# A two-layer trunk on one core: the pooling branch in pass 1 of the retention, and the first layer's last norm in the scheduler's order

## The chip, the cores and the metric

The kernel runs on one NeuronCore of a Trainium2 chip. The metric is the time of one execution on the device, in microseconds (us). Its engines are named as the profile names them: PE (TensorE, matrix products), DVE (VectorE), ACT (ScalarE), POOL (GpSimd) and SP (SyncE, which here issues DMAs). Each engine runs its own instructions in a fixed order and waits where a semaphore has not been reached yet.

## The reference

The input is a stream of 1024 tokens and 256 context tokens of width 1024, all in float32. Two layers follow each other; each adds two branches to the stream:

```python
for l in range(DEPTH):
    need_ctx = l < DEPTH - 1
    ax = modulate(rmsnorm(h, norm1_g[l]), mx[0], mx[1])
    ac = modulate(rmsnorm(hc, norm1_g[l]), mc[0], mc[1])
    yx, yc = mixing_layer(ax @ w_in[l], ac @ w_in[l], ...)
    h = h + mx[2] * (yx @ w_out[l])
    h = h + mx[5] * conv_ffn(modulate(rmsnorm(h, norm2_g[l]), mx[3], mx[4]), w_up[l], ..., w_down[l])
    if need_ctx:  # the same for hc, with mc and ac
        ...
return rmsnorm(h, final_g)
```

`mixing_layer` splits the projected columns over three kinds of heads: a pooling mixer (four groups of 64 columns, each with a centred mean over 2, 4, 8 or 16 tokens less the token itself, then a 64x64 product and a scale), a neighbourhood attention of six heads on a grid 64 columns wide, and a retention of six heads that runs over chunks of 128 tokens forwards and backwards. The retention rotates queries and keys by position, normalises each head's result and multiplies it by a silu gate. `conv_ffn` is a gated MLP of 2 x 2816 columns with a depthwise convolution over three tokens.

## The kernel before

Activations lie with their features on the 128 partitions and their tokens along the free axis. Tokens are cut in three parts: 0 and 1 are the two halves of 512 tokens of the stream, 2 is the context of 256. The last layer needs no context after its keys and values.

Products that need full precision are taken from pairs: a value is split in a rounded high part and the remainder (`xh` and `xl`, `wh` and `wl`, `ph` and `pl`), and each product is three matmuls, high by high, high by low, low by high (lines 194 to 196 for `gps`, the projections). A projection of one weight tile and one part of 512 tokens is 24 matmuls.

A layer runs like this: first norm, attention (each head's projections, then its softmax), retention, output projection (`ops`), second norm, then the MLP, whose up and down products are written in an order by hand and whose last two of 22 tiles of columns are done by plain down products (`dps`). The next layer's first norm is computed while these end.

**The retention** (`ret`) takes its six heads in three passes of two. A pass p consists of `keys` (load or project keys and values, rotate, transpose: `vps2`, `kps`; scale by decay: `kd`; the chunk sums: `pk`; the recurrence: `S`), `query` and `gate` (projections `gps` of the pass's columns), and `mix` (`pa`, the chunk's scores, `at`, these times a decay mask, `pf`, the query times the state, `py`, the scores times the values, then a norm per head in `tm` and a transpose `yps`).

**The pooling branch** is two calls of `pool_mean` and `pool_out`, for two groups of columns at a time. `pool_mean` loads a tile `pb` with a margin of zeros, adds shifted copies of it into the two halves `sa` and `sb` of a tile `sab` (line 559), corrects the eight columns at each end (572, 573), and writes mean less value back to `pb` (574). `pool_out` multiplies by the group weights (`pps`, line 582), scales on ACT (583) and stores to DRAM (584, 586). Two buffers are shared. `sab` has the tag of `kd`, with one buffer: it can be written when the last `pk` of the `keys` before it has read `kd`. `pb` has the tag of the raw keys and values `kw` and `vw`, with two buffers. The products `pps` and `py` share one PSUM buffer.

**What sets the order.** Outside the MLP a list scheduler places the instructions on each engine when the program is built, from estimated costs; the order in which the code emits them is a priority, not a rule. Inside `order`, a region in manual schedule that begins at the MLP, each engine keeps the order in which the code emits. The tail of the MLP lies inside it: `head(part, between)` emits the down products of one part, its residual `g` or `hd` (`acc_h`) and its squares, and between them the functions handed over, which compute the next norm of the part before: `st` (sums of squares by a product with ones, `nps`, and the power, `rs`), `sp` (the spread over the partitions, `dg` and `npb`), and `modulate` (`nt`, then `xh` on ACT and `xl` on DVE). The first projections of the next layer are `gps` again, and their first user is the copy `vt` on ACT (line 292), which frees the accumulator.

Of the kernel before, what the change touches and what calls it, by code (L numbers as in the profile page):

```python
# [7 lines left out]
F32 = mybir.dt.float32  # L8
F32R = mybir.dt.float32r
AF = mybir.ActivationFunctionType  # L10
# [9 lines left out]
KT = 8  # L20
# [19 lines left out]
NCH = 5  # L40
# [5 lines left out]
def tile_trunk(ctx, tc, xT, ctxT, cc, ccT, w_mod, w_mod0, colp, w_in, pool_bd, rpbU, lgp, w_out, w_up, w_down, fing,  # L46
# [297 lines left out]
    def mixing(l, X, mp):  # L344
# [186 lines left out]
        def ret():  # L531
# [207 lines left out]
            for p in range(3):  # L739
                if p == 0:  # L740
                    tables()
                kk = keys(p)
                q = query()
                gate(p)
                if p == 0:
                    for i in range(2):
                        pool_out(i, pool_mean(i))
                mix(p, *kk, q)
# [10 lines left out]
    def layer(l, X, hsrc):  # L759
# [24 lines left out]
        def hv(k, part):  # L784
            if part == 2:
                return hc[k]
            o, n = PARTS[part]
            return hs[0][k][:, o:o + n]
# [130 lines left out]
        def spread(part, pool, tag):  # L919
            pbs[part] = sums[part].spread(pool, tag)  # L920
# [350 lines left out]
        for ch in range(NCH):  # L1271
            for half in range(2):
                ps = {}
                tail = half == 1 and ch == NCH - 1
                if tail:
                    xpool[0] = wx
                for q in range(2):
                    ps["a", q] = psf.tile([128, 512], F32, tag="a", name="da")
                    bc = psf.tile([128, 1024], F32, tag="bc", name="dbc")
                    ps["c", q], ps["b", q] = bc[:, L], bc[:, R]  # L1280
                uc = {}
                nxt = ch + 1 < NCH
                for i, name in enumerate(names):
                    ui = UNITS.index(name) if name in PRODS else -1
                    if i == 0:
                        load_group(l, NF + 2 * ch + half + 1)
                    if ch == 0 and half == 0:
                        if name == "A11":
                            fetch(0, "T4")
                            reload((4, 5), 0)  # L1290
                            reload((6, 7), 1)
                        elif name == "A12":
                            reload((4, 5), 1)
                            reload((6, 7), 0)
                            if not last:
                                reload(range(4, 8), 2)
                    elif half == 0 and name == "A11":
                        fetch(ch, ops[6])
                    if half == 0 and not last:
                        j = 4 * ch + 4 + i - 3  # L1300
                        if 0 <= i - 3 < 4 and j < NF:
                            fetch_c(j)
                    if nxt and half == 0 and name == "A22":
                        fetch(ch + 1, ops[0])
                    if nxt and half == 1 and 0 <= ui < 6 and ui != 3:
                        fetch(ch + 1, ops[ui + (ui < 3)])
                    if half == 0 and 0 <= ui < 3:
                        convert(ch, ops[4 + ui])
                    if tail and name == "A11":
                        p = NF // 2 - 1  # L1310
                        raw_g = {(i, part): stage(g_dram[p][:, 2 * i + part]) for part in range(2) for i in range(2)}
                    if tail and ui > 2:
                        i, part = (ui - 3) % 2, (ui - 3) // 2
                        gl_[i, part] = pair(GTAG[("B11", "T1")[part]], raw_g[i, part])
                    wh, wl = [t.rearrange("p (k c) -> p k c", k=2) for t in weights()]
                    tick()
                    pop(1)
                    for q in range(2):
                        w = lambda j: (wh[:, j, 128 * q:128 * q + 128], wl[:, j, 128 * q:128 * q + 128])
                        if name != "A21":  # L1320
                            m, acc, start = PRODS[name]
                            product(ps[acc, q], w, G[ch, m], start)
                            r, part = TARGET[name]
                            acc_h(4 * half + 2 * r + q, part, ps[acc, q])
                        if not last and name[0] == "A":
                            r, kh = int(name[1]) - 1, int(name[2]) - 1
                            first = name in ("A11", "A21")
                            if first:
                                uc[q] = psg.tile([128, 512], F32, tag="g", name="dc")
                            product(uc[q][:, :C], w, [gcs[4 * ch + 2 * j + kh] for j in range(2)], first)  # L1330
                            if not first:
                                acc_h(4 * half + 2 * r + q, 2, uc[q])
                    if half == 0 and not last and 0 <= i - 4 < 4 and 4 * ch + i < NF:
                        convert_c(4 * ch + i)
                    if nxt and half == 1 and 0 <= ui < 4:
                        convert(ch + 1, ops[ui], nc.gpsimd)
                if ch == 0 and half == 0:
                    pop(len(todo))
                    put_all()
                    ust.close()  # L1340
                    wx = fp.enter_context(tc.tile_pool(name=f"wx{l}", bufs=1, side="right", reuse_waits="tile"))
        put_all()
        if not last:
            for i in range(2):
                gl_[i, 2] = gcs[NF - 2 + i]

        def down1(w, part, o, tag):
# [35 lines left out]
                for fn in between.get(o, ()):  # L1383
                    fn()

        late, copies = [], {}

        def settle():
            xl, t, b, xh = late.pop(0)
            nc.vector.scalar_tensor_tensor(xl, t, b, xh.bitcast(F32), op0=ALU.add, op1=ALU.subtract)  # L1390

        def modulate(part, ks):
            n = PARTS[part][1]
            cd = 1 if part == 2 else 0
            A, B = aff[1][cd][:, 0:8], mod[1][cd][:, 0:8]

            def go():
                for k in ks:
                    t = npl.tile([128, n], F32, tag="nt", name="nt", bufs=NT)
                    nc.vector.scalar_tensor_tensor(t, hv(k, part), A[:, k:k + 1], pbs[part][:, :n], op0=ALU.mult, op1=ALU.mult)  # L1400
                    xh, xl = xtile(part)
                    nc.scalar.activation(xh, t, AF.Identity, bias=B[:, k:k + 1])
                    late.append((xl, t, B[:, k:k + 1], xh))
                    if len(late) > 1:
                        settle()
                    Xn[k][part] = xh, xl
                    if part < 2:
                        o0 = PARTS[part][0]
                        nc.sync.dma_start(h_dram[:, k, o0:o0 + n], hv(k, part))
            return go  # L1410

        def final(part, *ks):
            o0, n = PARTS[part]
# [18 lines left out]
            return go  # L1432

        st = lambda part: lambda: sums[part].stats(psf, "bc")
        sp = lambda part: lambda: spread(part, psf, "bc")
        if not last:
            for cd in range(2):
                affine(1, 0, cd)
        head(0, {})
        if last:  # L1440
            head(3, {1: (st(0),), 5: (spread_copy(0, psf, "bc"),), 6: (final(0, 0),), 7: (final(0, 1),)})
            head(4, {1: (st(3), final(0, 2)), 2: (final(0, 3),), 3: (final(0, 4),), 4: (final(0, 5),),
                     5: (spread_copy(3, psg, "g"), final(0, 6, 7)), 6: (final(3, 0, 1),), 7: (final(3, 2),)}, 3)
            while held:
                held.pop(0)()
            sums[4].stats(psf, "bc")
            final(3, 3, 4, 5)()
            spread(4, psf, "a")
            final(3, 6, 7)()
            final(4, *range(KT))()  # L1450
        else:
            head(1, {1: (st(0),), 3: (sp(0), modulate(0, (0,))), 4: (modulate(0, (1,)),), 5: (modulate(0, (2,)),),
                     6: (modulate(0, (3,)),), 7: (modulate(0, (4,)),)})
            head(2, {2: (st(1), modulate(0, (5,))), 4: (modulate(0, (6,)),), 6: (modulate(0, (7,)),)})
            held.pop(0)()
            settle()
            prefetch()
            sp(1)()
            modulate(1, range(KT))()
            settle()  # L1460
            st(2)()
            sp(2)()
            modulate(2, range(KT))()
            settle()
        order.close()
        fp.close()
        return Xn

# [266 lines left out]
```

## Time and profile before

| | |
|---|---|
| time, median of 3 runs | 3043.04 us (3041.87 to 3045.44) |
| profiled execution | 3042.05 us |
| its span in the trace | 3040.2 us |
| mean granted clock of TensorE | 0.96 |
| busy: PE, DVE, ACT, POOL | 92%, 71%, 41%, 45% |
| retention of the first layer | about 440 to 690 us |
| tail of the first layer's MLP | about 1664 to 1736 us |
| retention of the second layer | about 2040 to 2250 us |

In a row of the timeline stand the start of an instruction (or of a run of like ones, with their count x), its duration, engine and line, output and inputs by the names in the program, the shapes, and in square brackets the idle time of the engine before it with what ended it. Neighbouring matmuls overlap: a row of 0.39 us follows the one before it by 0.23 us. PE rows of a later start with 0.63 us for the same matmul are at half clock. Lines are those of the kernel before.

### The profile page before, as it was taken

The page shows a single profiled execution, that of the slowest core. Times are in us where ns is not written, and L with a number is a line of the kernel's source. Part 1 is how long each engine was busy: PE and PEld are TensorE (multiplying, and loading weights), DVE is VectorE, ACT ScalarE, POOL GpSimd, SP SyncE. Part 2 cuts the span into 40 slices and gives each one's busy share as a digit, 9 for nine tenths or more (in the row PEclk, how much of TensorE's full clock was granted, in tenths as well). Part 3 has the DMA queues.
Part 4 walks back from the last instruction along what each step waited for, and adds up shares of the span by engine and source line. Part 5 has one row for each costly group of instructions (what it writes and reads, how often), then busy time and mean ns, then how long its engine had stood idle before and what let it go on. Part 6 is the DMA issues. An engine that isn't in the chain of part 4 may idle for free. (4 is left out here: it accounts for less than half of the span.)

```text
span 3040.2 us, 40234 instructions
## 1 busy us (share of the span) xinstructions
PE 2789.4 (92%) x14458; PEld 2336.4 (77%) x14458; DVE 2143.6 (71%) x3471; ACT 1248.3 (41%) x2401; POOL 1363.8 (45%) x900
## 2 busy tenths in 40 slices
PE   6789998989989999998999799998989899998998
PEld 4678877878768888887888688886777688887776
DVE  7887745462778777788787745447456777777997
ACT  4345542232444444434333355452223444444333
POOL 4335343323335445544554344444323455554554
PEclk8899998989999999999999899999989999999999
DMA  6343322032133434346332212121151233335442
GB/s 219 89 114 113 96 85 79 31 140 72 56 104 127 144 127 144 122 139 215 118 119 93 80 51 57 57 80 68 70 184 66 88 115 119 115 131 188 140 143 78
DMA packets 167738, 332.54 MB, mean 109 GB/s; under 512 B 49650, under 2 KB 62834, under 8 KB 167282
## 3 DMA queue, kind: packets, MB, share of 16 engines
q1 hardware_dynamic: 167252, 328.81, 33.0%
q8 instruction: 114, 1.87, 0.3%
q10 hardware_dynamic: 288, 1.18, 0.1%
q14 instruction: 84, 0.69, 0.1%
HBM read 255.72 MB, written 74.19 MB: 109 GB/s over the span
## 5 line engine op out<-in xcount | busy, mean ns | idle before, releaser
L962 PE MATMUL ua<-ph,wu 128*128 128x512 f32 x1408 | 449.5, 401 | 34.6 <-DVE ub L1062 16.2
L165 POOL TENSOR_TENSOR wu<-urb,wu 128x512 fp32r<-128x512 f32 x160 | 246.3, 1540 | 330.0 <-ACT wu L164 329.9
L165 POOL TENSOR_TENSOR wu<-ura,wu 128x512 fp32r<-128x512 f32 x192 | 305.4, 1591 | 156.1 <-ACT wu L164 155.9
L194 PE MATMUL gps<-xh,wh 128*128 128x512 f32 (+1 forms) x968 | 360.2, 373 | 14.6 <-ACT vt L292 7.7
L195 PE MATMUL gps<-xh,wl 128*128 128x512 f32 (+1 forms) x968 | 355.3, 367 | 0.0
L196 PE MATMUL gps<-xl,wh 128*128 128x512 f32 (+1 forms) x968 | 355.1, 367 | 0.0
L962 PE MATMUL ubc<-ph,wu 128*128 128x512 f32 x1056 | 331.8, 395 | 13.7 <-ACT wu L164 6.3
L962 PEld LDWEIGHTS ua<-ph,wu 128*128 128x128 f32 x1408 | 263.6, 191 | 98.0 <-ACT ut L1056 17.8
L449 POOL TENSOR_SCALAR P<-P,rs 128x640 f32<-128x640 f32 (+2 forms) x108 | 216.6, 2017 | 234.8 <-DVE rs L444 133.0
L165 POOL TENSOR_TENSOR wu<-S,wu 128x512 fp32r<-128x512 f32 x128 | 179.5, 1404 | 256.1 <-ACT wu L164 254.7
L962 PE MATMUL ua<-pl,wu 128*128 128x512 f32 x704 | 280.3, 398 | 0.2 <-DVE pl L858 0.2
L164 ACT CAST wu<-S 128x512 fp32r<-128x512 f32 x128 | 79.5, 621 | 424.9 <-DVE S L162 414.4
L962 PEld LDWEIGHTS ubc<-ph,wu 128*128 128x128 f32 x1056 | 198.4, 190 | 59.7 <-ACT wu L164 7.1
L186 POOL TENSOR_TENSOR wl<-wraw,wh 128x1024 fp32r<-128x1024 f32 x54 | 134.0, 2482 | 206.3 <-ACT wh L185 201.5
L194 PEld LDWEIGHTS gps<-xh,wh 128*128 128x128 f32 x968 | 185.9, 192 | 44.2 <-ACT vt L292 8.0
L962 PE MATMUL da<-ph,wu 128*128 128x512 f32 x640 | 204.2, 401 | 12.2 <-ACT wu L164 11.4
L962 PE MATMUL ubc<-pl,wu 128*128 128x512 f32 x528 | 207.4, 393 | 0.0
L195 PEld LDWEIGHTS gps<-xh,wl 128*128 128x128 f32 x968 | 185.6, 192 | 25.7 <-issue 1.0
L196 PEld LDWEIGHTS gps<-xl,wh 128*128 128x128 f32 x968 | 185.3, 191 | 26.0 <-issue 0.2
L164 ACT CAST wu<-urb 128x512 fp32r<-128x512 f32 x160 | 99.3, 622 | 181.2 <-DVE urb L162 151.2
L164 ACT CAST wu<-ura 128x512 fp32r<-128x512 f32 x192 | 118.9, 621 | 126.7 <-DVE ura L162 70.2
L962 PE MATMUL dbc<-ph,wu 128*128 128x512 f32 x480 | 150.7, 395 | 10.6 <-DVE c L1122 10.6
(304 smaller groups left out, 6882.4 us busy)
## 6 DMA issues: line engine op xcount, KB each, us to landing
gs<-g_dram SPq DMA_DIRECT2D x148, 256.0 KB, 2.8
wm<-in_w_mod_dram SPq DMA_DIRECT2D x56, 512.0 KB, 3.9
wmp<-in_w_mod_dram SPq DMA_DIRECT2D x112, 256.0 KB, 2.7
wraw<-in_w_in_dram SPq DMA_DIRECT2D x46, 512.0 KB, 3.6
ura<-in_w_up_dram SPq DMA_DIRECT2D x44, 512.0 KB, 4.3
urb<-in_w_up_dram SPq DMA_DIRECT2D x44, 512.0 KB, 5.2
g_dram<-gt SPq DMA_DIRECT2D x60, 256.0 KB, 3.2
g_dram<-c SPq DMA_DIRECT2D x44, 256.0 KB, 2.0
```

Source lines behind the costliest of these rows:

```text
L164: nc.scalar.copy(w[:, 0], b[name])
L165: nc.gpsimd.tensor_tensor(w[:, 1], b[name], w[:, 0].bitcast(F32), op=ALU.subtract)
L186: nc.gpsimd.tensor_tensor(wl.rearrange(flat), raw.rearrange(flat), wh.rearrange(flat).bitcast(F32), op=ALU.subtract)
L194: nc.tensor.matmul(ps[:, :n], wh[:, k], xh, start=k == 0, stop=False)
L195: nc.tensor.matmul(ps[:, :n], wl[:, k], xh, start=False, stop=False)
L196: nc.tensor.matmul(ps[:, :n], wh[:, k], xl, start=False, stop=k == KT - 1)
L449: nc.gpsimd.tensor_scalar(Pb[r][:, :w], Pb[r][:, :w], rs[:, r:r + 1], None, op0=ALU.mult)
L962: nc.tensor.matmul(ps, lt, rt, start=start and j == 0 and q == 0, stop=j == len(x) - 1 and q == 2, skip_group_check=True)
```

## The change

1. In `ret`, the pooling branch is emitted in pass 1, after `gate(1)` and before `mix(1)`; before, it was in pass 0. This holds for both layers.
2. In the first layer the region in manual order ends before the tail. The last tiles' activations are then loaded and split after the last unit of the MLP, where before this was woven into the last chunk. `head`, `modulate` and `settle` give way to `pipelined`: for each part all down products, with the adds of squares all on DVE, the sums, then the tiles of the part before by `modulated`, the function that the other norms use (for every third of the eight tiles k, `nt` gets its bias on ACT, `xh` is a copy on ACT and `xl` is made by POOL). The last layer keeps its tail.

```diff
@@ in ret
-                if p == 0:
+                if p == 1:
                     for i in range(2):
                         pool_out(i, pool_mean(i))
@@ in the MLP's down product
-                tail = half == 1 and ch == NCH - 1
+                tail = last and half == 1 and ch == NCH - 1
@@ behind it
         if not last:
+            order.close()
+            xpool[0] = wx
+            p = NF // 2 - 1
             for i in range(2):
+                for part in range(2):
+                    gl_[i, part] = pair(GTAG[("B11", "T1")[part]], stage(g_dram[p][:, 2 * i + part]))
                 gl_[i, 2] = gcs[NF - 2 + i]
...
+            acc_h(o, part, ps)
+            sums[part].add(hv(o, part), nc.gpsimd if last and o % 2 else nc.vector)
+
+        def pipelined(parts, head, tail):
+            prev = None
+            for part in parts:
+                head(part)
+                sums[part].stats(psf, "bc")
+                if prev is not None:
+                    tail(*prev)
+                prev = (part, sums[part].spread(psf, "bc"))
+            tail(*prev)
...
+        def down_tail(part, pb):
+            o0, n = PARTS[part]
+            res = modulated(1, 0, part, [hv(k, part) for k in range(KT)], pb, npl)
...
         else:
-            head(1, {1: (st(0),), 3: (sp(0), modulate(0, (0,))), 4: (modulate(0, (1,)),), 5: (modulate(0, (2,)),),
-                     6: (modulate(0, (3,)),), 7: (modulate(0, (4,)),)})
...
-            modulate(2, range(KT))()
-            settle()
-        order.close()
+            for cd in range(2):
+                affine(1, 0, cd)
+            pipelined(tail_parts, down_head, down_tail)
```

The function `modulated`, which the tail now calls, is not changed:

```python
for k in range(KT):
    t = pool.tile([128, n], F32, tag="nt", name="nt", bufs=NT)
    nc.vector.scalar_tensor_tensor(t, hs[k], A[:, k:k + 1], pb[:, :n], op0=ALU.mult, op1=ALU.mult)
    xh, xl = xtile(part)
    if k % 3 == 1:
        nc.scalar.activation(t, t, AF.Identity, bias=B[:, k:k + 1])
        nc.scalar.copy(xh, t)
        nc.gpsimd.tensor_tensor(xl, t, xh.bitcast(F32), op=ALU.subtract)
    else:
        nc.scalar.activation(xh, t, AF.Identity, bias=B[:, k:k + 1])
        nc.vector.scalar_tensor_tensor(xl, t, B[:, k:k + 1], xh.bitcast(F32), op0=ALU.add, op1=ALU.subtract)
```

The order of the instructions differs in three places on PE: the retention of the first layer, the tail, and the retention of the second layer. In the kernel before, PE's rows ahead of the first pooling product in pass 0 of the first layer are projections; the last 5 rows before it and those behind it:

```order
L195 MATMUL gps<-xh,wl 128x256
L196 MATMUL gps<-xl,wh 128x256
L194 MATMUL gps<-xh,wh 128x256
L195 MATMUL gps<-xh,wl 128x256
L196 MATMUL gps<-xl,wh 128x256
L582 MATMUL pps<-pb,pbd_4182 128x512 [waits DMAHW6_49,DMAHW1_49,DVE_49]
L700 MATMUL pa<-qr,kr 128x128 [waits DVE_49,PE_49]
L700 MATMUL pa<-qr,kr 128x128
```

With the change the same product stands on PE in pass 1, from the last chunk sums on (pbd_4182 and pbd_4183 are the group weights of the two pools):

```order
L657 MATMUL pk<-vv,kd 64x64 [waits Activation_49]
L657 MATMUL pk<-vv,kd 64x64 [waits DVE_49]
L657 MATMUL pk<-vv,kd 64x64 x12
L582 MATMUL pps<-pb,pbd_4182 128x512 [waits DMAHW4_49,DMAHW1_49,DVE_49]
L700 MATMUL pa<-qr,kr 128x128 [waits DVE_49,PE_49]
L700 MATMUL pa<-qr,kr 128x128
L582 MATMUL pps<-pb,pbd_4182 128x512 [waits Activation_49]
L700 MATMUL pa<-qr,kr 128x128 [waits DVE_49]
L700 MATMUL pa<-qr,kr 128x128
L707 MATMUL pf<-S,qr 128x128 [waits Pool_49]
L707 MATMUL pf<-S,qr 128x128 x3
L700 MATMUL pa<-qr,kr 128x128 [waits DVE_49]
```

No projection stands between the last `pk` and the first `pps` now. Behind these rows follow 3 and 4 further `pa`, the third `pps` of the first pool and then the first of the second pool (pbd_4183), again with no projection between. In the second layer the last `pk` and the first `pps` are neighbours in the same way; between its two pools stand two rows of three 256-column projection matmuls.

DVE's rows at that place, with the change:

```order
L666 SCALAR_TENSOR_TENSOR S<-S,cdec,pk 128x64 [waits PE_49]
L559 TENSOR_TENSOR sab<-pb 128x1311 [waits DMAHW5_49,DMAHW4_49,DVE_49]
L666 SCALAR_TENSOR_TENSOR S<-S,cdec,pk 128x64 [waits DVE_49]
L559 TENSOR_TENSOR sab<-sab 64x1309 [waits DVE_49]
L572 TENSOR_TENSOR sab<-sab,pcs 64x8 [waits DMAHW0_49]
L573 TENSOR_TENSOR sab<-sab,pcs 64x8
```

The first add into `sab` stands behind the step of the recurrence that waits for PE's last chunk sums; in pass 0 before it stood behind such a step too.

In the tail, ACT's last rows of the norm and the copy that frees the first accumulator of the next layer, before:

```order
L1402 ACTIVATE xh<-nt,mod_77 128x512 [waits DVE_49] x8
L1402 ACTIVATE xh<-nt,mod_78 128x256 [waits DVE_49] x8
L292 COPY vt<-gps 128x8x8x8 [waits DVE_49,PE_49,Pool_49]
L322 CAST qs<-gps 64x8x4x16 [waits PE_49,Pool_49]
L323 CAST kh<-gps 64x8x8x8 [waits DMAHW2_49]
```

and with the change, where two rows (279 and 280) make one `xh` of every third tile:

```order
L283 ACTIVATE xh<-nt,mod_78 128x256 [waits DVE_49] x2
L279 ACTIVATE nt<-nt,mod_78 128x256 [waits DVE_49,PE_49]
L280 CAST xh<-nt 128x256 [waits Activation_49]
L292 COPY vt<-gps 128x8x8x8 [waits DVE_49,Pool_49]
L322 CAST qs<-gps 64x8x4x16
```

The copy stays behind the last `xh` of part 2. Ahead of the tail, the four splits of part 0's and 1's last activations (`ph`) stand among ACT's last casts of `wu` in both kernels, but later in the changed one, and POOL's fills of `P` and `cb` for the next attention stand ahead of its last three subtractions for `wu`, where before they came behind them.

More of the change, by code (lines that the diff above doesn't have):

```diff
@@ L1384, in head @@
                     fn()
[L1386 to L1404, printed above, removed]
-                        settle()
[L1406 to L1410, printed above, removed]
+        copies = {}
@@ new lines, in down0 @@
+        def down0(w, part, o):
+            o0, pn = PARTS[part]
+            if o % 2:
+                ps = psf.tile([128, 512], F32, tag="a", name="dps")
+            else:
+                ps = psg.tile([128, 512], F32, tag="g", name="dps")
+            for i in range(2):
+                c0 = i * 512 + (o % 4) * 128
+                wh, wl = [t.rearrange("p a b -> p (a b)")[:, c0:c0 + 128] for t in w]
+                base = 1 if part > 2 else part
+                s0 = o0 - PARTS[base][0]
+                gh, gl = [t[:, s0:s0 + pn] for t in gl_[i, base]]
+                nc.tensor.matmul(ps[:, :pn], wh, gh, start=i == 0, stop=False)
+                nc.tensor.matmul(ps[:, :pn], wl, gh, start=False, stop=False)
+                nc.tensor.matmul(ps[:, :pn], wh, gl, start=False, stop=i == 1)
+            acc_h(o, part, ps)
+            sums[part].add(hv(o, part), nc.gpsimd if last and o % 2 else nc.vector)
@@ new lines, in pipelined, with down_head @@
+        def pipelined(parts, head, tail):
[7 more added lines that the diff above has]
+            tail(*prev)
+        def down_head(part):
+            for o in range(KT):
+                down0(ws[o // 4], part, o)
+        def down_tail(part, pb):
+            o0, n = PARTS[part]
+            res = modulated(1, 0, part, [hv(k, part) for k in range(KT)], pb, npl)
+            for k in range(KT):
+                Xn[k][part] = res[k]
+                if part < 2:
+                    nc.sync.dma_start(h_dram[:, k, o0:o0 + n], hv(k, part))
@@ L1434, in layer @@
         st = lambda part: lambda: sums[part].stats(psf, "bc")
[L1435 to L1439, printed above, removed]
         if last:
+            head(0, {})
             head(3, {1: (st(0),), 5: (spread_copy(0, psf, "bc"),), 6: (final(0, 0),), 7: (final(0, 1),)})
@@ L1450, in layer @@
             final(4, *range(KT))()
+            order.close()
         else:
-            head(1, {1: (st(0),), 3: (sp(0), modulate(0, (0,))), 4: (modulate(0, (1,)),), 5: (modulate(0, (2,)),),
-                     6: (modulate(0, (3,)),), 7: (modulate(0, (4,)),)})
[L1454 to L1462, printed above, removed]
-            modulate(2, range(KT))()
-            settle()
-        order.close()
+            for cd in range(2):
+                affine(1, 0, cd)
+            pipelined(tail_parts, down_head, down_tail)
         fp.close()
```

## The prediction

> **What bounds the kernel now.** I read the page first, for its busy times.
>
> ```profile
> span 3040.2 us, 40234 instructions
> PE 2789.4 (92%) x14458; PEld 2336.4 (77%) x14458; DVE 2143.6 (71%) x3471; ACT 1248.3 (41%) x2401; POOL 1363.8 (45%) x900
> ```
>
> TensorE is busy 92% of the span, and the change keeps its instructions. So the time moves by what TensorE's idle stretches gain or lose. Next, the busy time by stage: columns are PE, PEld, DVE, ACT, POOL (us busy, instructions), then TensorE's granted clock.
>
> ```profile
> 440.00:500.00 60.00, 45.75 (x292) 37.28 (x292) 44.94 (x89) 20.73 (x47) 27.70 (x34) 0.83 0.26 84
> 500.00:620.00 120.00, 120.00 (x746) 100.93 (x746) 54.08 (x116) 28.19 (x53) 41.44 (x26) 0.99 0.13 46
> 2050.00:2095.00 45.00, 34.64 (x210) 25.52 (x211) 34.17 (x59) 14.11 (x31) 19.02 (x27) 0.85 0.26 91
> 2095.00:2185.00 90.00, 90.00 (x564) 75.53 (x563) 43.60 (x83) 21.98 (x40) 33.44 (x20) 1.00 0.14 48
> 1690.00:1745.00 55.00, 36.91 (x165) 31.12 (x164) 41.11 (x69) 23.62 (x41) 21.85 (x22) 0.78 0.21 53
> ```
>
> Rows 1 and 3 are pass 0 of the retention in the two layers, with the pooling in it; rows 2 and 4 are pass 1, where TensorE does not stop at all. The last row is the tail of the first layer, where it stops for 18 of 55 us. The change moves the pooling from a stage with holes into one without, and reorders the tail. So I ask two things: what does the pooling cost where it lies now, and what covers it in its new place.
>
> **What the pooling costs in pass 0.** VectorE's sequence in the second layer, one pool after the other:
>
> ```profile
> 2068.60 2.23 DVE L559 TENSOR_TENSOR sab<-pb 128x1311 f32<-128x1311 f32 x1
> 2071.05 2.31 DVE L559 TENSOR_TENSOR sab<-sab 64x1309 f32<-64x1309 f32 x1
> 2075.82 1.28 DVE L574 SCALAR_TENSOR_TENSOR pb<-sab,pcs,pb 64x1024 f32<-64x1024 f32 x1
> 2077.52 3.70 DVE L559 TENSOR_TENSOR sab<-pb 128x1311 f32<-128x1311 f32 x1
> 2083.16 3.04 DVE L559 TENSOR_TENSOR sab<-sab 128x1305 f32<-128x1305 f32 x2
> 2086.78 2.60 DVE L574 SCALAR_TENSOR_TENSOR pb<-sab,pcs,pb 64x1024 f32<-64x1024 f32 x2
> ```
>
> Pool 0 runs from 2068.60 to 2077.10, 8.5 us; pool 1 is done at 2089.38, 12.3 us after it. TensorE meanwhile:
>
> ```profile
> 2063.80 0.92 PE L657 MATMUL pk<-vv,kd 128*64 128x64 f32 x24
> 2064.65 0.50 PE L194 MATMUL gps<-xh,wh 128*128 128x512 f32 x1
> 2075.44 0.39 PE L196 MATMUL gps<-xl,wh 128*128 128x512 f32 x1
> 2077.16 1.12 PE L582 MATMUL pps<-pb,pbd 128*128 128x512 f32 x2 [1.33 <-DVE pb L574]
> 2081.75 1.13 PE L700 MATMUL pa<-qr,kr 64*128 64x128 f32 x8 [2.32 <-DVE S L666]
> 2083.28 0.88 PE L707 MATMUL pf<-S,qr 64*128 64x128 f32 x5 [0.41 <-DVE S L666]
> ```
>
> Between the last `pk` and the first `pps` stand 48 projection matmuls (2064.65 to 2075.83, 11.2 us, 0.23 each). They cover pool 0 but for 1.33 us; the three holes make 4.06 us. In the first layer the same stretch has 96 of them, from 468.04, and loses one hole:
>
> ```profile
> 468.04 0.58 PE L194 MATMUL gps<-xh,wh 128*128 128x256 f32 x1
> 488.09 0.39 PE L195 MATMUL gps<-xh,wl 128*128 128x512 f32 x1
> 497.09 1.00 PE L700 MATMUL pa<-qr,kr 64*128 64x128 f32 x3 [4.10 <-DVE at L702]
> 501.13 0.63 PE L195 MATMUL gps<-xh,wl 128*128 128x512 f32 x1
> 471.22 2.23 DVE L559 TENSOR_TENSOR sab<-pb 128x1311 f32<-128x1311 f32 x1
> 480.92 2.19 DVE L574 SCALAR_TENSOR_TENSOR pb<-sab,pcs,pb 64x256 f32<-64x256 f32 x3
> 483.53 1.52 DVE L559 TENSOR_TENSOR sab<-pb 128x1311 f32<-128x1311 f32 x1
> 486.97 5.13 DVE L559 TENSOR_TENSOR sab<-sab 128x1305 f32<-128x1305 f32 x2
> 494.38 2.20 DVE L574 SCALAR_TENSOR_TENSOR pb<-sab,pcs,pb 64x256 f32<-64x256 f32 x3
> ```
>
> Pool 0 takes 11.9 us here (471.22 to 483.11), pool 1 ends 13.5 us later. After the hole the same matmul takes 0.63 us instead of 0.39: the clock was at half.
>
> **The pooling in pass 1.** Pool 0's first add writes `sab`, which shares its one buffer with `kd`, so it can't begin before the last `pk` of its pass. The order rows shown with the change have no projection matmul between that `pk` and `pps`: the cover of 11.2 and 17.5 us is gone, and VectorE's whole time for pool 0 becomes a hole. How long is it? The adds differ: 1.52 us at 483.53, but 2.23 and 3.70 at 2068.60 and 2077.52, when GpSimd was on a two-input operation:
>
> ```profile
> 2067.64 4.34 POOL L611 TENSOR_TENSOR qr<-qr,ru 128x512 f32<-128x512 f32 x2 [0.69 <-DVE ru L610]
> 2077.47 2.38 POOL L186 TENSOR_TENSOR wl<-wraw,wh 128x1024 fp32r<-128x1024 f32 x1 [5.49 <-ACT wh L185]
> ```
>
> In pass 1 the query's rotary is over by then, so I take pool 0 nearer its undisturbed time: second layer 8.5 less 1.4 for two adds at 1.52 gives 7.1, up to 8.5 (I take 8.0); first layer, which also has the context's columns and more short operations, 8 to 11.9 (I take 9.0). The Trainium skill says the same of the cause: "GPSIMD Engine Reference", section "Specifications", has GpSimd's SBUF interfaces shared with VectorE, in contention with VectorE instructions of two SBUF inputs. By that rule alone the low ends hold.
>
> Second hole: `pps` of pool 1 stands behind three `pps`, 12 `pa` and 4 `pf` in the first layer, and two `pps`, 12 `pa`, 4 `pf` and six 256-column `gps` in the second. At 0.14 us (1.13 for 8 `pa`), 0.23 for a 512-column `pps` and 0.12 for a `gps` of half the columns (estimates from the 0.23 above), that is 3 and 3.4 us of work. Pool 1 needs after pool 0: 13.5 less 2.1 (its pair of 5.13 at the 3.04 of the second layer) plus an estimated 0.7 for `at` operations now put between = 12; and 12.3 less 2.2 (3.70 at 1.52) plus 0.7 = 10.8. Holes: 9.0 and 7.4, with low ends of 7 and 6 where VectorE meets no GpSimd work, high ends of 10.5 and 9.
>
> What comes back: pass 0's holes, 4.1 and 4.06 us, because the work behind them no longer waits for VectorE. In pass 2 some projection work is now left to run between `kps` and `pk`, where before stood
>
> ```profile
> 2190.51 0.66 PE L729 MATMUL yps<-ident,tm 128*128 128x128 f32 x4 [2.19 <-DVE tm L726]
> 2192.01 1.09 PE L638 MATMUL vps<-ident,vw 128*128 128x128 f32 x8 [0.63 <-DVE yn L731]
> ```
>
> 2.8 us there, and an estimated 0.8 in the first layer. Sums: first layer 9.0 + 9.0 - 4.1 - 0.8 = +13.1 (10 to 18); second 8.0 + 7.4 - 4.06 - 2.8 = +8.5 (6 to 13). Together **+21.6, between 16 and 31**.
>
> **The tail.** TensorE's longest idle stretches there, and what runs last before the next layer's projections:
>
> ```profile
> 1697.69 1.42 PE L253 MATMUL nps<-ones,acc 128*128 128x1 f32 x8 [3.01 <-POOL acc L238]
> 1727.19 1.19 PE L265 MATMUL npb<-dg,ones 128*128 128x128 f32 x4 [5.18 <-DVE dg L264]
> 1736.09 0.79 PE L194 MATMUL gps<-xh,wh 128*128 128x512 f32 x1 [7.71 <-ACT vt L292]
> 1735.45 0.59 ACT L292 COPY vt<-gps 128x512 f32<-128x512 f32 x1 [0.63 <-DVE xl L1390]
> 1708.54 5.49 DVE L264 TENSOR_SCALAR dg<-ident,rs 128x128 f32<-128x128 f32 x4
> 1709.53 0.74 POOL L376 MEMSET P<- 128x768 f32 x1
> 1716.31 0.75 DVE L1390 SCALAR_TENSOR_TENSOR xl<-nt,mod,xh 128x512 fp32r<-128x512 f32 x1
> 1734.86 0.48 DVE L1390 SCALAR_TENSOR_TENSOR xl<-nt,mod,xh 128x256 fp32r<-128x256 f32 x1 [0.18 <-ACT xh L1402]
> ```
>
> The last hole ends with ACT's copy of `vt` at 1735.45, which frees the accumulator. It stands in ACT's queue behind every `xh` of parts 1 and 2, and these wait for VectorE, which makes each tile's `nt` and `xl` by itself, up to 1735.34. After the change the copy still stands behind all of them, but three of eight `xl` per part go to GpSimd: 3 x 0.75 + 3 x 0.48 = 3.7 us less in that stretch. The four small `dg` tiles took 5.49 us, where a whole 128x512 `xl` takes 0.75, while GpSimd filled `P` and `cb` for the attention; these fills now stand earlier in its order: up to 4.7. Against it, 14 adds of squares go from GpSimd to VectorE, 7 x 0.75 + 7 x 0.48 = 8.6 us by the same rows, most of it while VectorE waited for the down projection's matmuls. Net I put the copy at about 1728: **-7.5 us, between 0 and -13**. The sum of the three holes, 15.9, is about the most that any order could return there.
>
> **The clock.** In the first layer all from 497.09 to past 501.13 ran at half speed after the hole of 4.10 us: 4 us or more, which loses 2 to 3. Now each layer has a pair of long holes. What runs between the two is covered by the wait, so one stretch per layer counts: 0 more in the first, an estimated 1 to 2 more in the second, as much less in the tail. I take 0, with -3 to +6. The Trainium skill has a rule that speaks louder: "TensorE: Matmul & The Clock Gate", Part 1, gives half clock after an idle window of some 3.4 us. By it each of the four new holes halves the clock for at least such a window. The 4.10 us hole agrees.
>
> **Sum.** Against the profiled execution of 3042.05: + 21.6 - 7.5 + 0 = 3056. The median of the runs is 3043.04, 1 us above it, within their spread; I keep **3056**.
>
> **Rivals.**
> *The tail repays the pooling* (not slower). The point that decides is whether the first `gps` of part 1 still waits for `vt`. If the copy comes by 1722, 13.5 us are back, and 4 more of the 12 that the clock lost in this stretch (55 x 0.22); with the pooling's low end, 16, it is 3042 + 16 - 17.5 = 3040.5. For it: the largest single waits of the tail lie in this chain. Against: the copy keeps its place behind 16 tiles of work.
> *The tail turns worse.* The loads of the last down tiles are now made ready behind the last unit, with four casts on ACT and the fills of `P` on GpSimd now ahead of `wu` work that TensorE waits for, and VectorE has the adds. If that costs 4 us instead of saving 7.5, the time is 3042 + 21.6 + 4 = 3068.
> *The clock after every hole.* If the work behind each of the four holes runs at half speed as after the hole at 497.09, 3 us lost each, less the 3 that pass 0 lost so: 9 more, 3065.
>
> **How the numbers follow.** Forecast 0.53, tail repays 0.14, tail worse 0.18, clock 0.15. The forecast's own range is 3047 to 3065; down to the first rival's and up to the second's gives **3042 to 3069**, with about 2 in 10 left out. Some 0.2% (6 us) is what a measurement of this kernel can tell from no change. Slower by more: 0.86 of the forecast and both last rivals, 0.79. Within: 0.13 of the forecast and half of the first rival, 0.14. Faster: the rest, 0.07.
>
> **What would show it.** In pass 1 of each layer, two idle stretches of TensorE: one of 7 to 12 us ahead of the first `pps`, released by `pb` L574, and one of 6 to 10 ahead of pool 1's. The wait at 497.09 gone. The row of the copy of `vt` near 1728, counted from the first `dps`. The forecast is wrong if these two stretches are under 4 us, or if pass 2 gives back more than 6 us.

## The result

The changed kernel took 3063.76 us (median of 4 runs, 3058.22 to 3071.11) against 3042.45 for the kernel before on the same occasion: a ratio of 1.0064, with a 95% interval of 1.0043 to 1.0085. A second set of 5 runs gave 1.0071 (1.0056 to 1.0087). It is slower by some 20 us. The forecast was 3056, with a range of 3042 to 3069.

The page of the changed kernel:

```profile
span 3062.8 us, 40241 instructions
PE 2810.0 (92%) x14458; PEld 2356.5 (77%) x14458; DVE 2129.4 (70%) x3476; ACT 1251.8 (41%) x2410; POOL 1352.1 (44%) x895
```

TensorE has the same instructions and 20.6 us more busy time: much of the loss does not show as idle time at all. To see where it lies, I cut both traces at the same instructions: the first retention with its output projection, the MLP of the first layer, the tail, the second layer up to its MLP, that MLP, and the last stage (from the first `dps` of the last layer). Busy times by these windows, before:

```profile
452.00:788.00 336.00, 311.27 (x1835) 260.92 (x1834) 169.12 (x340) 96.89 (x187) 114.56 (x91) 0.92 0.25 87
788.00:1664.00 876.00, 827.74 (x4230) 698.96 (x4229) 692.45 (x958) 353.78 (x593) 414.81 (x271) 0.98 0.38 126
1664.00:1751.40 87.40, 66.91 (x305) 55.76 (x304) 60.69 (x102) 35.39 (x59) 29.08 (x27) 0.84 0.27 82
1751.40:2321.30 569.90, 534.67 (x3116) 453.09 (x3115) 304.35 (x640) 231.77 (x538) 235.44 (x142) 0.97 0.26 84
2321.30:2994.80 673.50, 633.24 (x2705) 511.99 (x2704) 557.95 (x627) 303.52 (x472) 362.42 (x239) 0.98 0.37 120
2994.80:3033.50 38.70, 31.48 (x205) 27.75 (x203) 27.85 (x55) 15.52 (x32) 13.45 (x16) 0.99 0.20 74
```

and after:

```profile
452.00:798.30 346.30, 314.87 (x1832) 263.88 (x1831) 164.68 (x339) 96.41 (x187) 110.19 (x91) 0.90 0.24 84
798.30:1675.40 877.10, 829.86 (x4230) 701.18 (x4229) 692.96 (x960) 355.19 (x593) 422.91 (x279) 0.98 0.39 127
1675.40:1756.70 81.30, 64.88 (x306) 54.03 (x305) 58.69 (x105) 38.12 (x68) 17.54 (x14) 0.85 0.22 73
1756.70:2335.00 578.30, 542.09 (x3117) 461.37 (x3116) 295.75 (x640) 231.47 (x539) 233.45 (x142) 0.94 0.25 83
2335.00:3010.00 675.00, 634.82 (x2705) 513.23 (x2704) 558.76 (x626) 303.56 (x472) 361.64 (x239) 0.98 0.36 120
3010.00:3056.20 46.20, 40.06 (x205) 36.45 (x203) 27.05 (x55) 15.62 (x32) 13.33 (x16) 0.75 0.17 62
```

The first retention costs 10.3 us more, the tail gives back 6.1, the second layer's mixing costs 8.4 more. The last stage, whose code and order the change leaves alone, costs 7.5 more, all of it at a lower granted clock (0.99 to 0.75). The two MLPs make up the rest of the difference, 1.1 and 1.5 us. TensorE's idle time (a window less its busy time) grew by 6.7 us in the first retention and by only 1.0 in the second layer's mixing: most of that layer's loss is work at a lower clock.

The pooling in pass 1, PE's rows: the first layer, then the second. (In the kernels with added lines the line numbers are shifted: L582 becomes L586 or L589, and L574 becomes L578.)

```profile
549.52 1.15 PE L657 MATMUL pk<-vv,kd 128*64 128x64 f32 x28
558.86 2.08 PE L582 MATMUL pps<-pb,pbd 128*128 128x512 f32 x2 [8.19 <-DVE pb L574]
568.52 1.22 PE L582 MATMUL pps<-pb,pbd 128*128 128x256 f32 x2
571.67 2.07 PE L582 MATMUL pps<-pb,pbd 128*128 128x512 f32 x2
575.68 0.58 PE L194 MATMUL gps<-xh,wh 128*128 128x256 f32 x1
2143.67 2.08 PE L582 MATMUL pps<-pb,pbd 128*128 128x512 f32 x2 [7.29 <-DVE pb L574]
2154.23 0.58 PE L194 MATMUL gps<-xh,wh 128*128 128x256 f32 x1
```

The first hole is there in both layers, 8.19 and 7.29 us. The second pool's product (571.67) has no idle time before it. Instead all rows from the first `pps` on run at half clock, until the projections have run for a while. One `pps` is written as two rows' worth (x2) and takes 2.07 us here; 1.02 at full clock. The window over this work says it in one row: 15.71 of 17.07 us busy, clock 0.50.

```profile
558.24:575.31 17.07, 15.71 (x47) 9.83 (x48) 13.37 (x26) 4.10 (x7) 2.49 (x2) 0.50 0.10 39
```

VectorE's adds for the two pools of the first layer were undisturbed; GpSimd was idle for 36 us until 572.75:

```profile
550.91 1.52 DVE L559 TENSOR_TENSOR sab<-pb 128x1311 f32<-128x1311 f32 x1
552.65 1.52 DVE L559 TENSOR_TENSOR sab<-sab 64x1309 f32<-64x1309 f32 x1
563.40 3.06 DVE L559 TENSOR_TENSOR sab<-sab 128x1305 f32<-128x1305 f32 x2
```

### The profile page after: what moved, and what is told of

Same layout as the page of the kernel before. It is cut to its first block, busy times and chain, and to the rows that moved or that the text cites. A ratio compares the mean times of both kernels' runs of the same rounds, so it can differ in the third digit from the quotient of the medians.

```text
span 3062.8 us, 40241 instructions
## 1 busy us (share of the span) xinstructions
PE 2810.0 (92%) x14458; PEld 2356.5 (77%) x14458; DVE 2129.4 (70%) x3476; ACT 1251.8 (41%) x2410; POOL 1352.1 (44%) x895
## 5 line engine op out<-in xcount | busy, mean ns | idle before, releaser
L962 PE MATMUL dbc<-ph,wu 128*128 128x512 f32 x480 | 150.9, 396 | 10.3 <-DVE c L1122 10.3
```

The lines of the kernel that those rows point to most:

```text
L962: nc.tensor.matmul(ps, lt, rt, start=start and j == 0 and q == 0, stop=j == len(x) - 1 and q == 2, skip_group_check=True)
```

## The experiments

### The two parts apart

The tail alone (pooling in pass 0):

```diff
-                if p == 1:
+                if p == 0:
```

> The pooling is back in pass 0; only the tail of the first layer is in the scheduler's order. Theory A (the parts add up): the tail repays what the trace of the changed kernel shows between the last unit of the first MLP and the next attention, 11.5 - 5.3 = 6 us, so about 3036. Rival B (the tail gained only because everything in it ran 11 us later than its loads): no gain, 3041 to 3045. Both retentions should read as before: holes of 4.1 us at 497 and 1.3 + 2.3 + 0.4 us near 2077.

The ratio was 0.9988 (0.9974 to 1.0002). The pooling alone (the kernel before, with `p == 1`):

> Only the pooling is moved to pass 1; the tail is the one of the kernel before. Theory A: +10.5 in the first layer and +9.7 in the second, +20, so about 3062; the changed kernel's median is this less the 6 us of the tail, plus what the clock does in the last 30 us. Rival B: the 8 us that the changed kernel's profile lost in the last 30 us, in code that the change leaves alone, come from the change as well, and then 3068 to 3072 here, and the last half-clock stretch is long in this profile too. Under A that stretch is a matter of chance from run to run.

The ratio was 1.0072 (1.0049 to 1.0096). The parts add up: -0.12% and +0.72%, 0.60% together, against 0.64 and 0.71 measured for both. By stages, the first retention takes 335.9 to 336.1 us in seven of the eight profiles with the pooling in pass 0 (338.6 in the eighth), and 346.0 to 346.6 in four with it in pass 1 and nothing added there. But in the pooling's profile the last stage took 44.8 us, in the tail's own 46.1: rival B stayed open, and its long half-clock stretch came with the pooling in pass 0, too. So I took two programs once more. The kernel before:

> The kernel before once more, for a second profile of the same program. If stages of unchanged order differ from the first profile by some us, always with a half-clock stretch that is longer or shorter, then the differences of that size between two single profiles belong to the clock and not to the change; if the profiles agree within 1 us in every stage, the 8 us that the changed kernel lost in its last 30 us need another cause.

Its ratio to itself was 0.999 (0.9975 to 1.0006). Its last stage took 38.5 us again, its first retention 336.0. But the tail, which is the same program, differs by 4.5 us (83.0 instead of 87.4, at clock 0.90 instead of 0.84), and the second layer's mixing by 3.2 the other way:

```profile
1664.50:1747.50 83.00, 62.76 (x307) 52.15 (x306) 58.31 (x102) 35.37 (x59) 28.92 (x27) 0.90 0.28 86
```

So a difference of 3 to 5 us between single profiles of one stage need not be an effect of an edit, where the clock differs. The tail's old order took 83.0, 87.5 and 89.9 in three profiles, the new one 79.8 to 81.3 in ten.

The changed kernel once more:

> The changed kernel once more, beside the other kernels of this call. The stages of two profiles that differ only in the pooling's place give +10.3 us in the first retention, about +7 in the second and -5 in the tail, +12. Theory M (the rest of the +20 seen was the last stage, which fell to half clock in both profiles of that session): if the last stage takes 38.5 us here, the profile is about 3052 to 3056; if it takes 45 or more, 3059 to 3064. Rival N (the change makes the last stage slow): 45 us or more again, as in its first profile, and no slower last stage where the pooling is in pass 0.

Its last stage took 44.8 us, its profile 3059.9. That is the branch of 45 us of theory M, and rival N isn't excluded by it: three of three profiles with this pooling in both layers and no added work have the slow stage. Of the two with matmuls added in pass 1 (below), one has it (44.8) and one hasn't (39.6). What makes it slow came out of the clock, below.

### What makes the hole

```diff
-            W = T + C + 4 * PADX
+            W = 1280 if last else T + C + 4 * PADX
...
+                if last:
+                    sa = ra.tile([128, W], F32, tag="sa", name="sab", bufs=1)
+                    sb = rp.tile([128, 10, 2, 64], F32, tag="S", name="sab", bufs=2).rearrange("p a b c -> p (a b c)")
```

> The changed kernel, but in the second layer the sums of the pooling have buffers of their own (one new tile, and one buffer of the recurrence's states) instead of the buffer of kd, and the pooled rows are 1280 columns long instead of 1312. The pool's adds then need not wait for the last pk of pass 1, and the order has 33 projection matmuls ahead of its last 13 and 9 and 18 more around the second pool. Theory G (the shared buffer is what made the hole): the idle 7.3 us and the half clock behind it in the second layer are gone; that layer's +9.7 us falls to 0 to 2, so the ratio to the kernel before falls from 1.0064 to about 1.0035. Rival H (VectorE is the limit in pass 1 wherever the pool's 20 us stand): other holes of together 5 us or more in this stage, ratio 1.005 to 1.0065.

The ratio was 1.0028 (1.0014 to 1.0042). The second layer's mixing took 571.5 us, like the kernels with the pooling in pass 0 and shared buffers (566.9 to 574.6), with the pooling still in pass 1; the first layer kept its 346.2. PE at the two pools:

```profile
2130.25 1.13 PE L586 MATMUL pps<-pb,pbd 128*128 128x512 f32 x2 [1.45 <-DVE pb L578]
2151.10 1.12 PE L586 MATMUL pps<-pb,pbd 128*128 128x512 f32 x2 [0.86 <-DVE pb L578]
```

Holes of 1.45 and 0.86 us instead of 7.29, at full clock. Theory G holds for this hole: the buffer shared with `kd` made it. The price was that the pool can't begin before the last `pk`, with no projections left.

The ratio alone doesn't show the size of that gain. This profile's last stage took 38.5 us, and the edit opened another hole, ahead of pass 0 of the second layer, where the kernel before and the changed one wait 1.61 us:

```profile
2062.12 2.15 PE L642 MATMUL vps<-ident,vw 128*128 128x128 f32 x9 [11.04 <-DMA vw<-r_dram]
```

So the 571.5 us contain a gain at the pool and a new loss, and are not the price of pass 1 by itself.

### Hole or clock

```diff
+                    if i == 0 and part == 0:
+                        for j in range(24):
+                            nc.tensor.matmul(ps, warm[0], X[0][0][0], start=True, stop=True)
```

> The changed kernel with 24 projection-like matmuls (fp32r, 128x512, 0.23 us each) put ahead of the first pooling product of each layer, released by pool 0's first add; their result is overwritten. A small copy on VectorE and one buffer go with them. By this the scheduler also moves the second pool's products behind some 30 projection matmuls. Theory C (the larger part of the price in pass 1 is the half clock behind the hole): no half clock at 558 to 579 and 2143 to 2159, 3.5 to 9 us less per layer, so 3045 to 3056. Rival D (the hole alone is the price, and the second pool's wait would show as idle time once the clock is full): the same time within 4 us, 3058 to 3064.

The twin has six matmuls of `rope_sb`, plain float32:

> As the kernel with 24 projection-like matmuls in the hole and in the same order on TensorE, but with 6 plain float32 matmuls of 128x512 there (1.0 us each at full clock by the pps row). Theory E (plain float32 work doesn't hold the clock up, as 17 us of busy pps, pa and pf rows at half clock after the hole suggest): the clock still falls to half in the hole and stays there until projections run, 4 to 10 us slower than its twin. Rival F (any busy TensorE holds the clock): as fast as its twin within 2 us.

The ratios were 1.0043 (1.0024 to 1.0062) and 1.0041 (1.0026 to 1.0056). Neither theory C nor E came out. Rows of the first (first layer), then of the twin (first and second layer):

```profile
553.00 5.74 PE L588 MATMUL pps<-xh,warm 128*128 128x512 f32 x24 [2.13 <-DVE warm L565]
561.83 1.19 PE L707 MATMUL pa<-qr,kr 64*128 64x128 f32 x4 [1.69 <-DVE S L673]
```

```profile
558.15 5.42 PE L588 MATMUL pps<-rope_sb,warm 128*128 128x512 f32 x12 [2.13 <-DVE warm L565]
568.06 2.07 PE L589 MATMUL pps<-pb,pbd 128*128 128x512 f32 x2
2147.25 7.11 PE L588 MATMUL pps<-rope_sb,warm 128*128 128x512 f32 x12 [2.13 <-DVE warm L565]
2155.15 1.16 PE L707 MATMUL pa<-qr,kr 64*128 64x128 f32 x8
```

The hole shrank to 2.1 us in both. In the first layer the next wait, 1.69 us, brought the half clock all the same, and it stayed for 17.07 us in both kernels, until projections had run. That layer's retention took 349.5 and 349.4 us, 3 more than in the changed kernel: the second pool's products moved behind 34 projections, and `py` came later for it. In the second layer no such wait follows; the clock came back while the added matmuls still ran, plain float32 or not, and `pa` ran at full speed from then on (8 in 1.16 us; 2.05 in the changed kernel). Theory E is refuted: six float32 matmuls of 512 columns in a row brought the clock back. Rival D is right on the sum: filling the hole alone wins nothing in the first layer. The twins' second layers took 581.7 and 575.6 us, one at half clock for 20 us of pass 2 and the other for 7, so I read no gain from them. Both ratios lie below the changed kernel's 1.0064 and 1.0071, with intervals that overlap; what the twin's profile has less lies in its second layer and its last stage (39.6 us), where the clock differs. The twin also gives the price of a plain float32 matmul of 512 columns at full clock: 5.42 us for six, 0.90 each, four times the 0.23 of a projection's.

### The tail's term

```diff
-            if k % 3 == 1:
+            if third and k % 3 == 1:
...
-            res = modulated(1, 0, part, [hv(k, part) for k in range(KT)], pb, npl)
+            res = modulated(1, 0, part, [hv(k, part) for k in range(KT)], pb, npl, third=False)
```

> The tail alone in the scheduler's order (pooling in pass 0), but all eight xl tiles of a part made by VectorE, none on GpSimd. Theory I (the tail gains because VectorE's last stretch is shorter by the tiles it hands over, 3.7 us of the prediction's sum): the time from the first dps to the copy of vt goes from 63.9 to about 67.6 us; the time, about 3 to 4 us above the tail alone. Rival J (it gains because the down products no longer stand among the norm's waits: they took 29.5 us instead of 41.3): 64 to 65 us, no difference in time.

From the first `dps` to the copy of `vt`: 65.6 us, against 63.9 with the tiles on GpSimd and 71.5 and 67.0 in the two profiles of the kernel before. The ratio was 0.9986 (0.9973 to 0.9999), no different from the tail with GpSimd. It lies between I (67.6) and J (64 to 65), nearer to J: 1.7 us of the gain comes from the tiles handed over. The rest goes with the new order, in which the down products took 29.5 us in a row instead of 41.3 (38.4 in the second profile) among the norm's waits; no run takes that order apart further.

TensorE's idle time separates order and clock better than the stage's length. It was 20.5 and 20.2 us in the two profiles of the kernel before, 16.4 to 16.5 in two each of the changed kernel and of the tail alone, and 18.2 with all tiles on VectorE (the window 82.50 less 64.29 busy). So the new order saves some 4 us of idle time, 1.8 of them by the tiles; what the profiles differ by beyond that is the clock.

```profile
1660.40:1742.90 82.50, 64.29 (x307) 53.91 (x306) 60.86 (x114) 33.78 (x59) 6.40 (x5) 0.86 0.22 72
```

### The last stage

```diff
+        def warm(n):
+            def go():
+                ps = psf.tile([128, 512], F32, tag="a", name="wps")
+                for j in range(n):
+                    nc.tensor.matmul(ps, ws[0][0].rearrange("p a b -> p (a b)")[:, 0:128], gl_[0, 0][0], start=True, stop=True)
+            return go
...
-            head(3, {1: (st(0),), ...
-            head(4, {1: (st(3), final(0, 2)), ...
+            head(3, {1: (warm(4), st(0)), ...
+            head(4, {1: (warm(8), st(3), final(0, 2)), ...
```

> The tail alone in the scheduler's order (pooling in pass 0), and in the last layer's tail 4 and 8 fp32r matmuls of 128x512, with a result that is not read, put ahead of two sums of squares for which TensorE waits 1.0 and 2.2 us. Theory K (the last 30 us fall to half clock when an activity window catches the second of these holes, and stay there): from the second hole on full clock, the last stage as in the trace of the kernel before or 1 us better, 3 to 6 us less than the tail alone in most runs, and less spread. Rival L (which windows go slow has nothing to do with these holes): no difference, and the long half-clock stretch stays.

The ratio was 0.9972 (0.9959 to 0.9986), and the last stage 38.7 us. To compare on one chip, this kernel and the tail alone were run again:

> The tail alone, with 12 matmuls in the holes of the last stage, on the same chip as the tail alone. Theory K (they keep the clock up in the last stage): that stage at 38.5 to 39 us again, and 1 to 5 us faster than the tail alone by the median, as often as that one falls. Rival L (chance): no difference, 45 us in some profiles.

> The tail alone in the scheduler's order once more, on the same chip as the two kernels built on it. By the stages 81.3 us instead of 83 to 87.5: 3 to 5 us faster than the kernel before, ratio 0.9984 to 0.999. Its last stage is 38.5 or 46 us by chance; 46 in its first profile.

The tail alone came to 0.9978 (0.9966 to 0.9991), this kernel to 0.9975 (0.9964 to 0.9987): no difference, since this time the tail alone had its last stage at 38.5 us. Here both beat the kernel before, by 0.2%, which the tail's first runs did not show clear of noise; the added matmuls are not shown to win time. What they do to the hole is plain. The hole in the changed kernel, in the tail alone (second profile), and with the matmuls:

```profile
3036.25 0.98 PE L253 MATMUL nps<-ones,acc 128*128 128x1 f32 x4 [2.17 <-POOL acc L238]
```

```profile
3011.19 0.61 PE L253 MATMUL nps<-ones,acc 128*128 128x1 f32 x4 [2.17 <-POOL acc L238]
```

```profile
3009.82 0.61 PE L253 MATMUL nps<-ones,acc 128*128 128x1 f32 x4 [0.34 <-POOL acc L238]
```

The same hole of 2.17 us is followed by half clock in the first and not in the second. The granted clock changes only at steps of 3.41 us. Cut at these steps, the changed kernel around the hole (3034.08 to 3036.25), then the tail alone (3009.02 to 3011.19):

```profile
3032.91:3036.32 3.41, 1.04 (x7) 0.84 (x7) 1.02 (x3) 1.75 (x4) 2.42 (x3) 1.00 0.22 82
3036.32:3039.73 3.41, 3.41 (x16) 3.41 (x17) 1.79 (x4) 0.40 (x1) 0.71 (x1) 0.50 0.40 154
```

```profile
3006.78:3010.19 3.41, 2.03 (x15) 1.62 (x14) 2.08 (x5) 2.17 (x5) 1.73 (x2) 1.00 0.22 82
3010.19:3013.60 3.41, 2.41 (x21) 2.41 (x21) 1.77 (x4) 0.38 (x1) 1.65 (x3) 1.00 0.22 85
```

Where the whole hole lies in one step, TensorE is busy for 1.04 of 3.41 us, and the next step runs at half clock. Where a step's end divides it, 2.03 and 2.41 us are busy, and the clock stays. In eleven profiles without the added matmuls in this stage this holds throughout: with 1.65 to 2.17 us of the hole in one step (5 profiles) the stage took 44.8 to 46.1 us; with 1.20 or less (6 profiles), 38.5 to 39.6. So for this hole the time that has passed before decides, to a fraction of 3.41 us.

The idle share of a step is not the whole rule, though. The first hole of this stage, 1.02 us long, shows it in the changed kernel:

```profile
3022.67:3026.08 3.41, 2.41 (x20) 2.42 (x21) 1.98 (x5) 0.91 (x3) 1.08 (x2) 1.00 0.00 0
3026.08:3029.49 3.41, 2.76 (x14) 2.46 (x12) 1.59 (x5) 1.29 (x4) 2.81 (x4) 0.50 0.00 0
```

TensorE is busy for 2.41 us of the step, as in the last row above, and yet half clock follows, for one step. In six of the eleven profiles this hole began within 0.6 us of a step's start and one step at half clock followed; in the other five it began 1.7 to 2.0 us into a step and none did. Where a hole lies in the steps separates the cases again; what the chip counts within a step stays open.

### The two ideas together

The tail alone, the matmuls in the last stage, and the pooling's own buffers in the second layer, in pass 0:

> The tail alone with the matmuls in the last stage, and in the second layer buffers of the pooling's own, the pooling being in pass 0. Theory G (the shared buffer sets when the pool may begin): the three holes of 1.3, 2.3 and 0.4 us at the pool in the second layer shrink to under 1.5 together, 2 to 5 us faster than the same without, ratio to the kernel before 0.996 to 0.9975. Rival H (VectorE is the limit in pass 0 too): the same time, other holes at kd or S.

The ratio was 1.0002 (0.999 to 1.0014): no gain. The three holes at the pool are gone, as G has it. But a new one of 10.8 us opened ahead of the retention, as in the run with the pooling in pass 1:

```profile
2052.21 2.15 PE L642 MATMUL vps<-ident,vw 128*128 128x128 f32 x9 [10.79 <-DMA vw<-r_dram]
```

The values of pass 0 arrive late. With two places of the pooling and the same hole, it comes with the buffers and not with the pass. In the run with the pooling in pass 1 the load was issued at 2052.5 us, against 2032.5 in the changed kernel. That the new buffers push it back behind memory which the attention still holds is my reading; no run tested it.

## Why the prediction was right, and where it was not

**The direction and the bounds held**: 3064 lies in the range, above the 3056 of the sum and at the upper end of the likeliest case's own range. That it came so near is in part luck. The three places that the change touches gave 10.3 + 7.5 - 6.1 = 11.7 us where the sum had 14.1; most of the rest lies in the last stage, which the sum did not have.

**First hole: right.** Forecast 9.0 and 8.0 us with low ends of 8 and 7.1; measured 8.19 and 7.29. The low ends were the true values, for the reason given with them: with GpSimd idle the adds took 1.52 us. That agrees with "GPSIMD Engine Reference", section "Specifications", of the Trainium skill, on the shared SBUF interfaces.

**Second hole: the wrong mechanism with nearly the right size.** I forecast 9.0 and 7.4 us of idle time between the pools and found none ahead of the second pool in either layer, only 0.7 and 0.3 ahead of the first `pa`. The prediction named two stretches under 4 us as a sign that it is wrong: the second stretch was, so its mechanism failed here. Two steps failed. The price of `pps` was taken from the projections' 0.23 us, and is 0.90; the prediction's own row of 1.12 us at 2077.16 is one such product. And the clock term said that what runs between the holes at half speed is covered by the wait. It was, but the waiting time was filled with it, and the half clock went on behind it until 578.7 and 2159. From the first `pps` at 558.86 that is 19.9 us at half speed with 0.7 idle, so 9.6 us lost, where I had 9.0 of idle time: nearly the same size by chance.

**The retentions.** First layer: +10.3 against +13.1. The wait at 497.09 is gone, and with it the half clock behind it, which had cost some 3.2 us (6.46 busy at clock 0.50, from 496.72 to 503.55). An estimate from these rows, 8.2 + 9.6 - 4.1 - 3.2 = 10.5, meets the measured value. Second layer, by the profiles with shared buffers: the median of seven profiles with the pooling in pass 0 is 570.7, of three in pass 1 578.2, so +7.5 against +8.5. What came back in pass 2 of the second layer, 2.8 us, did come back: the only waits over 2 us left there are 2.38, 4.16 and 2.88, which stood there before as well (2.37, 4.25, 2.88). Two holes of 1.0 and 1.7 us ahead of the projections of pass 0 are new.

**The tail: the size near, the reason half right.** -7.5 forecast; 71.5 to 63.9 from the first `dps` to `vt` is -7.6 between the two first profiles, -3.1 against the second of the kernel before. The whole stage is 6.1 us shorter in the mean (86.8 in three profiles, 80.7 in ten), and the time 0.12% (not clear of noise) and 0.22% lower, 4 to 7 us. The holes I counted on moved rather than closed:

```profile
1731.77 1.20 PE L265 MATMUL npb<-dg,ones 128*128 128x128 f32 x4 [7.00 <-DVE dg L264]
1739.99 0.80 PE L194 MATMUL gps<-xh,wh 128*128 128x512 f32 x1 [7.02 <-ACT vt L292]
```

The copy of `vt` still ends the stage. The 3.7 us for tiles handed to GpSimd measured 1.7. The other 2 us or so of saved idle time go with the new order as a whole, which I hadn't priced, and the rest of the difference between the profiles is clock.

**The clock: the term that was mis-sized.** I took 0, with -3 to +6. In pass 1 of the first layer the half clock cost 9.6 us, which took the place of the second hole. The last stage alone was +6 to 7.5 in both profiles of the changed kernel, in a place that the prediction did not look at. It completes the sum: 10.3 + 7.5 - 6.1 + 6.9 (the two slow stages' mean of 45.5 less 38.6) = 18.6, against 19.5 and 21.6 by the two ratios. The rival "the clock after every hole" had the nearest number, 3065, but not this way: in pass 1 only one stretch per layer ran at half speed, and the last stage wasn't in it. Whether the changed kernel falls into the slow last stage always, or mostly by chance, stays open: it did in three of three profiles with its pooling, and the tail alone in one of two.

On the rule of the Trainium skill, "TensorE: Matmul & The Clock Gate", Part 1: the windows of about 3.4 us that run free of the kernel are in every trace here. An idle window as a whole is not needed here: steps of 3.41 us with 2.4 us without work, and in six profiles with 1.0, were followed by half clock, while others with 1.4 were not. The way back, after a busy window, is not confirmed for all work: `pps`, `pa` and `pf` kept TensorE busy for 15.71 of 17.07 us and the clock stayed at half.

## What to carry to other kernels

Before moving a branch to a stage where TensorE has no holes, ask what releases its first instruction and which independent matmuls stand between that release and its use; if a shared buffer ties it to the end of the stage's own chain, its whole length becomes a hole. A buffer of its own removes that hole, but look at what the buffer delays: here a load came late by it, and neither kernel with such buffers beat the kernel before. Price each matmul from a row of its own type, and count the half clock that follows a hole as part of the hole. And compare single profiles stage by stage together with the granted clock: a stage whose order is unchanged can differ by 7 us by when its hole falls.

## What was new about the hardware

A hole of 2.17 us cost either nothing or some 5 to 6.5 us (stages of 44.8 to 46.1 us against 39.6, the longest of the others), by where it fell in the clock's steps of 3.41 us: half clock followed when one step held 1.65 us or more of it, in 5 profiles, and never with 1.20 or less, in 6. The busy time of the step is not enough to tell: with 2.41 us busy, one step was followed by half clock and another was not. Once at half speed, the last stage's mixture of 256-column matmuls and one-column sums stayed there for 13.65 us in three profiles and to its end, some 20 us later, in two, though the same mixture at full speed held the clock in the other profiles. The attention-like products `pa` and `pf` with `pps` did the same in pass 1: at full clock they kept it (2154 to 2163 us in the twin), at half they didn't get it back in 17 us, while a step of projections did, and so did six plain float32 matmuls of 512 columns.
